# A hand-written TensorE order for the differential-attention mixer of a one-core float32 network

## The chip, the cores and the metric

The kernel is one program on one core of a Trainium2 chip. Its time is the device time of one execution, in microseconds. The core has five engines, each with its own instruction stream: TensorE (PE, matmuls and transposes), VectorE (DVE), ScalarE (ACT), GpSimd (POOL) and SyncE (SP, which issues DMAs). An engine runs its stream in order. A semaphore makes an instruction wait for another engine, and everything behind it on that engine waits too.

## The reference, cut to what matters

Two blocks with convolution, attention and feed-forward layers come first. Then a second network of two layers runs on T = 272 tokens (16 learned meta tokens and 256 real ones) of width 1024. Its first layer is a gated feed-forward, the mixer that is changed here, and another feed-forward; a sparse-attention mixer and more feed-forwards follow. The mixer is differential attention with 8 heads. Each head has two queries and two keys of width 64, and one value of width 128:

```python
def _diff_attention(h, pos, cid, w_in, qk_norm, lam, subln, lambda_init, rel_bias):
    q, k, v = jnp.split(h @ w_in, [2 * A_HEADS * A_HD, 4 * A_HEADS * A_HD], axis=-1)
    q = _rms_norm(q.reshape(bsz, t, A_HEADS, 2, A_HD), qk_norm[0])
    k = _rms_norm(k.reshape(bsz, t, A_HEADS, 2, A_HD), qk_norm[1])
    ...
        logits = jnp.einsum("bqhmd,bkhmd->bmhqk", qb, k).astype(jnp.float32) * scale + bias
        p = jax.nn.softmax(jnp.where(visible, logits, NEG_INF), axis=-1)
        pd = p[:, 0] - lam_full * p[:, 1]
        return jnp.einsum("bhqk,bkhe->bqhe", pd.astype(v.dtype), v)
    ...
    o = _rms_norm(o, subln) * (1.0 - lambda_init)
    return o.reshape(bsz, t, A_HEADS * A_VD)
...
h = h + mix @ w_out[layer]
```

Everything is float32. Chunks of 64 tokens limit what a query sees; the 16 meta queries see only the meta tokens.

## The kernel before, in words

**Dense work.** A float32 product is three matmuls (`mm3`, L212 to L214): weights and activations are each split into a high part (`wh`, `xh`) and a rest (`wl`, `xl`), and wh.xh, wh.xl and wl.xh are summed in one PSUM bank. One step is 128 x 128 weights against 272 columns. Weights stream through the kernel in a fixed plan: SP loads a chunk of 2048 columns (`raw`), ACT casts a piece of up to 1024 (`wh`, L187), DVE, or POOL for a few pieces, subtracts (`wl`, L189). `take` hands out the next piece, `ahead` splits one more, four pieces ahead of use.

**The mixer** (`diff_mix`) works head by head. `prep(h)` projects the head's queries and keys (two tiles of 8 `mm3` steps), scales them (`hx`, L831), loads two bias tiles, squares (`sq`, POOL, L843), sums squares over 64 rows by a matmul with a block of ones (L847), and normalises: two logarithms and two exponentials on ACT (L848, L849), then DVE products into `nu` (L850 to L852) and `qk` (L856). `values(h)` projects the values (8 steps), scales them into `vx` (L863), and transposes them in three pieces (L868 to L870). `attend(h)` makes the scores of both softmaxes (L220), adds the bias and takes minima (L895), exponentials on ACT, their weighted difference (L911), four transposes (`probs_t`, L977 to L980), and the product with the values (L916). After each odd head, `sub_norm` normalises a pair of heads (sum of squares by a matmul with ones, L929) and splits the result into `y`, the input of the output projection. `meta` does the same for the 16 meta queries of several heads at once.

**PSUM.** The mixer has eight banks by tag: mm 2, s 2, t 1, n 2, o 1 (L788). The tag n is used by the lambda product, each `n` sum of squares, the value transposes, the meta work, and the last pair's norm. A new bank of a tag waits until the one from two uses earlier has been read.

**The order.** The heads are written as a loop: `prep` two heads ahead (LAG = 2), `attend(h)`, `prep(h + 2)`, `values(h + 1)`. A scheduler with a model of the engines then decides each engine's final order, so that on PE the blocks of different heads lie among each other. `out_proj` (L376) takes the output projection in two passes over the eight result tiles: `WO_PASSES[2]` names the inputs (heads) of each pass, and each pass adds into the residual `X` (L388). The first pass here uses heads 0 to 5, the second 6 and 7.

## Time and profile before

| | |
|---|---|
| three runs | 1722.18, 1720.2, 1721.84 us; median 1721.84 |
| profiled execution | 1716.95 us, span 1715.2 us |
| granted TensorE clock, mean | 0.994 |
| busy share of the span | PE 98%, DVE 64%, ACT 52%, POOL 22% |
| DMA | 287.56 MB, mean 168 GB/s |
| chain that ended last | PE 92%, DVE 4%, ACT, issue and DMA 1% each |

The profile is of one execution; its span is the time between the first and the last instruction, and the execution lasts 1.75 us longer. PE is busy nearly throughout, so the places where it waits are few and can be listed. A matmul's row lasts longer than the distance to the next row, because matmuls are pipelined: costs of PE work are read from the distance of starts.

### The profile page before, as it was taken

What the parts mean: (1) busy time and instruction counts of PE and PEld (TensorE: products, weight loads), DVE (VectorE), ACT (ScalarE), POOL (GpSimd) and SP (SyncE); (2) the same over time, 40 slices, a digit from 0 to 9 for tenths busy, and PEclk for the clock granted to TensorE, in tenths of its full rate; (3) what the DMA queues carried; (4) which work ended last, traced back from release to release, by engine and by line L of the source; (5) the groups of instructions that cost most, each with busy time, mean ns of one, the idle gap of its engine ahead of it and who ended that gap; (6) DMA issues with size and microseconds to landing.
All of it is one profiled execution on the core that took longest, in us unless ns stands there. A gap on an engine that the chain in (4) does not pass through costs nothing.

```text
span 1715.2 us, 32923 instructions
## 1 busy us (share of the span) xinstructions
PE 1678.1 (98%) x13474; PEld 1633.1 (95%) x13474; DVE 1103.9 (64%) x1808; ACT 895.9 (52%) x1554; POOL 375.6 (22%) x402
## 2 busy tenths in 40 slices
PE   7999999999999999999999999999999989999999
PEld 7999999998899999999988999999999977899999
DVE  7767666565766566655788766556665576666652
ACT  6545445476544555444566544445444457754441
POOL 3013220011322013211421222211221224432210
PEclk9999999999999999999999999999999999999999
DMA  8456655432555545445642454554454333335551
GB/s 282 167 195 225 229 185 185 172 124 99 174 195 179 191 172 174 177 176 180 193 127 89 147 174 174 174 182 171 177 177 174 124 126 126 124 136 186 183 192 69
DMA packets 59495, 287.56 MB, mean 168 GB/s; under 512 B 12064, under 2 KB 22816, under 8 KB 27472
## 3 DMA queue, kind: packets, MB, share of 16 engines
q1 hardware_dynamic: 58512, 284.80, 47.6%
q8 instruction: 106, 1.74, 0.4%
q10 hardware_dynamic: 832, 0.66, 0.1%
q14 instruction: 45, 0.37, 0.1%
HBM read 284.34 MB, written 5.53 MB: 169 GB/s over the span
## 4 chain that ended last, share of the span: by engine, by line
PE 92%; DVE 4%; ACT 1%; issue 1%; DMA 1%; POOL 0%; SPq 0%; ACTq 0%; DVEq 0%; POOLq 0%
PE mm L212 21%; PE mm L213 21%; PE mm L214 21%; PE z L214 8%; PE z L212 8%; PE z L213 8%; DVE wl L189 1%; PE s L1177 1%; PE o L220 1%; PE z L220 1%; DVE xl L229 1%; PE o L916 1%; DMA X<-in_xT_dram 1%; PE s L220 1%; PE n L847 0%
## 5 line engine op out<-in xcount | busy, mean ns | idle before, releaser
L187 ACT CAST wh<-raw 128x1024 fp32r<-128x1024 f32 (+1 forms) x521 | 540.5, 1040 | 634.3 <-PE mm L213 418.2
L189 DVE TENSOR_TENSOR wl<-raw,wh 128x1024 fp32r<-128x1024 f32 (+1 forms) x513 | 631.7, 1233 | 315.3 <-ACT wh L187 312.6
L212 PE MATMUL mm<-xh,wh 128*128 128x256 f32 (+2 forms) x1768 | 510.0, 289 | 5.4 <-DVE X L388 2.2
L213 PE MATMUL mm<-xl,wh 128*128 128x256 f32 (+2 forms) x1768 | 506.1, 286 | 4.0 <-DVE xl L229 3.7
L214 PE MATMUL mm<-xh,wl 128*128 128x256 f32 (+2 forms) x1768 | 506.3, 286 | 0.0
L212 PEld LDWEIGHTS mm<-xh,wh 128*128 128x128 f32 (+1 forms) x1768 | 333.4, 189 | 11.7 <-issue 2.8
L213 PEld LDWEIGHTS mm<-xl,wh 128*128 128x128 f32 (+1 forms) x1768 | 332.8, 188 | 8.0 <-DVE xl L229 4.9
L214 PEld LDWEIGHTS mm<-xh,wl 128*128 128x128 f32 (+1 forms) x1768 | 333.6, 189 | 1.2 <-issue 0.6
L214 PE MATMUL z<-xh,wl 128*128 128x256 f32 (+1 forms) x1088 | 311.0, 286 | 0.0
L213 PE MATMUL z<-xl,wh 128*128 128x256 f32 (+1 forms) x1088 | 309.9, 285 | 0.0
L212 PE MATMUL z<-xh,wh 128*128 128x256 f32 (+1 forms) x1088 | 309.6, 285 | 0.0
L212 PE MATMUL mm<-gh,wh 128*128 128x256 f32 (+1 forms) x1056 | 300.5, 285 | 0.0
L214 PE MATMUL mm<-gh,wl 128*128 128x256 f32 (+1 forms) x1056 | 299.5, 284 | 0.0
L213 PE MATMUL mm<-gl,wh 128*128 128x256 f32 (+1 forms) x1056 | 299.5, 284 | 0.0
L344 POOL TENSOR_TENSOR es<-es,r 128x256 f32<-128x256 f32 (+1 forms) x110 | 157.1, 1428 | 483.8 <-ACT es L343 483.8
L214 PEld LDWEIGHTS z<-xh,wl 128*128 128x128 f32 x1088 | 205.5, 189 | 0.2
L212 PEld LDWEIGHTS z<-xh,wh 128*128 128x128 f32 x1088 | 205.2, 189 | 0.0
L213 PEld LDWEIGHTS z<-xl,wh 128*128 128x128 f32 x1088 | 204.8, 188 | 0.0
L213 PEld LDWEIGHTS mm<-gl,wh 128*128 128x128 f32 x1056 | 199.2, 189 | 0.0
L214 PEld LDWEIGHTS mm<-gh,wl 128*128 128x128 f32 x1056 | 198.5, 188 | 0.0
L212 PEld LDWEIGHTS mm<-gh,wh 128*128 128x128 f32 x1056 | 198.4, 188 | 0.0
L345 DVE TENSOR_TENSOR ea<-z,es 128x256 f32<-128x256 f32 (+1 forms) x132 | 57.1, 433 | 96.1 <-PE z L214 52.1
(362 smaller groups left out, 1793.3 us busy)
## 6 DMA issues: line engine op xcount, KB each, us to landing
raw<-in_gu_dram SPq DMA_DIRECT2D x132, 1024.0 KB, 4.8
raw<-in_wd_dram SPq DMA_DIRECT2D x66, 1024.0 KB, 4.8
raw<-in_wo_dram SPq DMA_DIRECT2D x13, 1024.0 KB, 4.8
raw<-in_aw_dram SPq DMA_DIRECT2D x12, 1024.0 KB, 4.8
raw<-in_a_in_dram SPq DMA_DIRECT2D x9, 1024.0 KB, 5.3
nb<-scr SPq DMA_DIRECT2D x32, 136.0 KB, 2.4
scr<-relrow SPq DMA_DIRECT2D x16, 271.5 KB, 5.2
raw<-in_mkv_dram SPq DMA_DIRECT2D x4, 1024.0 KB, 4.8
```

The lines of the kernel that those rows point to most:

```text
L187: self.nc.scalar.copy(h[:, :c], t[:, x : x + c])
L189: eng.tensor_tensor(l[:, :c], t[:, x : x + c], h[:, :c].bitcast(F32), ALU.subtract)
L212: mm(out, wh, xh, start=first, stop=False, skip_group_check=chk)
L213: mm(out, wh, xl, start=False, stop=False, skip_group_check=chk)
L214: mm(out, wl, xh, start=False, stop=last, skip_group_check=chk)
L220: self.nc.tensor.matmul(out, w, x, start=start, stop=stop, skip_group_check=True)
L229: self.nc.vector.scalar_tensor_tensor(l, src, col, h.bitcast(F32), ALU.mult, ALU.subtract)
L344: nc.gpsimd.tensor_tensor(s, s, r, ALU.mult)
L345: nc.vector.tensor_tensor(a, B[:, :cols], s, ALU.mult)
L916: nc.tensor.matmul(os[0][:, e * S + oc.start : e * S + oc.stop], v, pr[:, pc], start=e == 0 and i == 0, stop=e == 1 and i == 3, skip_group ...
L1177: nc.tensor.matmul(s[:, c], q[:, k, qc], ckg[:, k, k0 : k0 + n], start=k == 0, stop=k == 1)
```

## The change

The functions are cut in smaller ones (`project`, `normalise`, `value`, `turn`, `scores`, `probs`, `apply`, `pair_norm`, `meta_probs`, `meta_apply`, `meta_norm`), and these are called in a written sequence. While `in_order` is set, every PE instruction goes through a wrapper (`Ordered`) that keeps it in program order; in the changed kernel all PE instructions therefore carry the line L141. The other engines stay with the scheduler. The output projection takes heads 0 to 3 in its first pass and 4 to 7 in its second; the first pass's eight steps stand between the work of heads 6 and 7, and the second pass's first four tiles are done in two halves. The meta work is grouped 4 + 4 instead of 6 + 2, with its product in a bank of tag t. Outside the mixer PE's calls go through the wrapper with `in_order` off; the rest of the code is the same.

```diff
-    [[0, 1, 2, 3, 4, 5], [6, 7]],
+    [[0, 1, 2, 3], [4, 5, 6, 7]],
...
+class Ordered:
+    def __init__(self, net, eng):
+        self.net, self.eng = net, eng
+    def __getattr__(self, name):
+        f = getattr(self.eng, name)
+        def call(*args, **kw):
+            ins = f(*args, **kw)
+            if self.net.in_order:
+                self.net.tc.keep_in_program_order(ins)
+            return ins
+        return call
...
+    def wo_pass(self, i, p, y, cols, res, tags):
+        ks = WO_PASSES[i][p]
+        n = len(ks)
+        per = wo_pieces(n)
+        ws, banks = {}, {}
+        def step(m, lo=0, hi=n):
+            if not lo:
+                if m % per == 0:
+                    ws[m // per] = self.take(f"wo{i}_{p}", per * n)
+                banks[m] = self.bank(tags[m % len(tags)])
+            w = ws[m // per]
+            for j in range(lo, hi):
+                c = m % per * n + j
+                self.mm3(banks[m][:, :cols], (w[0][:, c], w[1][:, c]), (y[0][:, ks[j], :cols], y[1][:, ks[j], :cols]),
+                         j == 0, j == n - 1, chk=True)
+            if hi == n:
+                self.nc.vector.tensor_tensor(res[m], banks[m][:, :cols], res[m], ALU.add)
+                if m % per == per - 1:
+                    self.ahead()
+        return step
...
-            def prep(h):
+            def project(h):
...
+                nc.gpsimd.tensor_tensor(sq, x, x, ALU.mult)
+                qks[h] = x, sq, nbs
+            def normalise(h):
+                x, sq, nbs = qks.pop(h)
...
-            def values(h):
+            def value(h):
...
+            def turn(h):
+                vx = vxs[h % 2]
                 b = self.bank("n")[:, : 3 * P].rearrange("p (a b) -> p a b", a=3)
-                nc.tensor.transpose(b[:, 0], vx[:, 48 : 48 + P], self.ident)
-                nc.tensor.transpose(b[:, 1], vx[:, 48 + P :], self.ident)
-                nc.tensor.transpose(b[:48, 2], vx[:, :48], self.ident)
+                self.pe.transpose(b[:, 0], vx[:, 48 : 48 + P], self.ident)
+                self.pe.transpose(b[:, 1], vx[:, 48 + P :], self.ident)
+                self.pe.transpose(b[:48, 2], vx[:, :48], self.ident)
...
-            def attend(h):
+            os, qks, vs, pms, prs, sqs = {}, {}, {}, {}, {}, {}
+            def scores(h):
                 qk, nbs = qks.pop(h)
-                vr, vq = vs.pop(h)
-                e = h % 2
-                pm = []
+                pm = pms[h] = []
...
-                if h == NH - 1:
-                    meta(6, NH)
-                (L, _), (L1, s1) = pm
+            def probs(h):
+                (L, _), (L1, s1) = pms.pop(h)
                 for qc, k0, n, c, tt in SEGS:
                     nc.vector.scalar_tensor_tensor(L[:, c], L1[:, c], s1[:, 2 + tt : 3 + tt], L[:, c], ALU.mult, ALU.add)
-                pr = self.probs_t(L, pt, self.bank("t"))
+                prs[h] = self.probs_t(L, pt, self.bank("t"))
+            def apply(h):
+                vr, vq = vs.pop(h)
+                e, pr = h % 2, prs.pop(h)
...
+                    sq = self.t(pt, [P, 2 * S], "osq", bufs=1)
+                    nc.scalar.activation(sq, os[0], AF.Square)
+                    sqs[h] = os[0], sq
+            def pair_norm(h):
+                o, sq = sqs.pop(h)
+                yh, yl = (c[:, h - 1 : h + 1, NM:] for c in y)
+                sub_norm(o, sq, yh, yl, 2, S, "t" if h < NH - 1 else "n", (pt, "o", 2 * S))
...
-                o = self.bank("n")
+                prs["meta"] = ph
+            def meta_apply(h0, h1):
+                n, ph = h1 - h0, prs.pop("meta")
+                o = self.bank("t")
...
-            for h in range(LAG):
-                prep(h)
-            values(0)
-            for h in range(NH):
-                attend(h)
-                if h + LAG < NH:
-                    prep(h + LAG)
-                if h + 1 < NH:
-                    values(h + 1)
-                if h == 5:
-                    meta(0, 6)
-            self.out_proj(2, y, T, Xf, ("mm", "s"))
+                    self.pe.matmul(o[:, c], vm[:NM, h0 + h], ph[:, c], start=True, stop=True)
+                sq = self.t(self.p_ev, [P, T], "ea")[:, : n * NM]
+                nc.scalar.activation(sq, o[:, : n * NM], AF.Square)
+                sqs["meta"] = o, sq
+            def meta_norm(h0, h1):
+                sub_norm(*sqs.pop("meta"), y[0][:, h0:h1, :NM], y[1][:, h0:h1, :NM], h1 - h0, NM, "n", None)
+            project(0)
+            self.in_order = True
+            project(1)
+            normalise(0)
+            value(0)
+            normalise(1)
+            turn(0)
+            for h in range(6):
+                scores(h)
+                project(h + 2)
+                probs(h)
+                if h == 4:
+                    meta_probs(0, 4)
+                value(h + 1)
+                if h == 4:
+                    meta_apply(0, 4)
+                apply(h)
+                if h == 4:
+                    meta_norm(0, 4)
+                normalise(h + 2)
+                turn(h + 1)
+                if h % 2:
+                    pair_norm(h)
+            early = self.wo_pass(2, 0, y, T, Xf, ("mm",))
+            late = self.wo_pass(2, 1, y, T, Xf, ("s", "s", "mm", "mm"))
+            scores(6)
+            value(7)
+            early(0)
+            early(1)
+            probs(6)
+            scores(7)
+            turn(7)
+            early(2)
+            apply(6)
+            early(3)
+            early(4)
+            probs(7)
+            meta_probs(4, NH)
+            early(5)
+            meta_apply(4, NH)
+            apply(7)
+            meta_norm(4, NH)
+            pair_norm(7)
+            early(6)
+            early(7)
+            for m in range(4):
+                late(m, 0, 2)
+            for m in range(4):
+                late(m, 2, 4)
+            for m in range(4, KD):
+                late(m)
+            self.in_order = False
```

**PE, a head in the middle of the loop.** Before, the two sums of squares of one head (`n<-sq,blk`) are followed by the rest of the probabilities' transposes and by scores; the value transposes (`ident,vx0` into `n`) stand 27 rows later, behind projection steps.

```order
L847 MATMUL n_1465_10301<-sq_1462_10297,blk_93 128x272
L847 MATMUL n_1466_10306<-sq_1462_10297,blk_93 128x272
L978 MATMUL t_1446_10197<-ident_91,L10_1374_9756 128x128
L979 MATMUL t_1446_10197<-ident_91,L10_1374_9756 128x128
L980 MATMUL t_1446_10197<-ident_91,L10_1374_9756 128x128
L220 MATMUL s_1474_10358<-qk_1436_10127 128x272
...
L868 MATMUL n_1472_10350<-ident_91,vx0_1370_9752 128x128
L869 MATMUL n_1472_10350<-ident_91,vx0_1370_9752 128x128
L870 MATMUL n_1472_10350<-ident_91,vx0_1370_9752 48x128
```

Now the sums of squares of head 3 come behind the product of head 1 with its values, and the transposes of head 2's values directly behind them, ahead of head 2's scores. Of the tag n's two banks the two sums take both, and the transposes take the next.

```order
L141 MATMUL o_1434_10139<-pr_1430_10106,vm_1366_9748 128x128
L141 MATMUL o_1434_10139<-pr_1430_10106,vn0_1367_9749 128x128
L141 MATMUL n_1437_10146<-sq_1428_10097,blk_93 128x272
L141 MATMUL n_1438_10151<-sq_1428_10097,blk_93 128x272
L141 MATMUL n_1440_10162<-ident_91,vx1_1371_9753 128x128 x2
L141 MATMUL n_1440_10162<-ident_91,vx1_1371_9753 48x128
L141 MATMUL s_1443_10171<-qk_1411_9985 128x144
L141 MATMUL s_1442_10170<-qk_1411_9985 128x144
```

What moved: the transposes stand directly behind the sums of squares that use the same tag, and the next head's scores stand behind the transposes.

**PE, the last two heads.** Before, the meta norm (`n<-ea,ones`), head 6's product, head 7's probabilities and its values' transposes stand together, and the first projection step (`mm<-xh,wh`) comes after the meta transposes.

```order
L929 MATMUL n_1599_11107<-ea_1598_11105,ones_92 128x96
L916 MATMUL o_1608_11153<-pr_1607_11151,v_1593_11076 128x256
...
L916 MATMUL o_1608_11153<-pr_1607_11151,vn0_1367_9749 128x128
L977 MATMUL t_1626_11255<-ident_91,L10_1374_9756 128x128
...
L980 MATMUL t_1626_11255<-ident_91,L10_1374_9756 128x128
L868 MATMUL n_1612_11189<-ident_91,vx1_1371_9753 128x128
L869 MATMUL n_1612_11189<-ident_91,vx1_1371_9753 128x128
L870 MATMUL n_1612_11189<-ident_91,vx1_1371_9753 48x128
L950 MATMUL n_1619_11231<-ident_91,ml_1365_9746 16x16 x2
L212 MATMUL mm_1633_11282<-xh_1363_9744,wh_1576_10999 128x272
```

Now steps of the projection (`mm<-xl,wh`, `mm<-xh,wl`) stand ahead of head 6's probabilities (`L00`) and again behind the transposes of head 7's values.

```order
L141 MATMUL mm_1611_11187<-xl_1364_9745,wh_1578_11007 128x272
L141 MATMUL mm_1611_11187<-xh_1363_9744,wl_1579_11008 128x272
L141 MATMUL t_1614_11207<-ident_91,L00_1372_9754 128x128 x4
L141 MATMUL s_1617_11215<-qk_1596_11091 128x144
L141 MATMUL s_1616_11214<-qk_1596_11091 128x144
...
L141 MATMUL n_1620_11239<-ident_91,vx1_1371_9753 128x128 x2
L141 MATMUL n_1620_11239<-ident_91,vx1_1371_9753 48x128
L141 MATMUL mm_1622_11247<-xh_1363_9744,wh_1580_11011 128x272
L141 MATMUL mm_1622_11247<-xl_1364_9745,wh_1580_11011 128x272
L141 MATMUL mm_1622_11247<-xh_1363_9744,wl_1581_11012 128x272
```

What moved: the output projection's first pass has come forward from behind head 7 to between the blocks of heads 6 and 7.

**DVE, the first two heads.** Before, one head's `nu`, the values of head 0 and the second head's `nu` stand as here.

```order
L851 SCALAR_TENSOR_TENSOR nu_1387_9842<-nu_1387_9842,nt_1388_9843 128x544
L831 TENSOR_TENSOR hx_1392_9861<-mm_1395_9889,r_1359_9722 128x272
L852 SCALAR_TENSOR_TENSOR nu_1387_9842<-nu_1387_9842,nt_1388_9843 128x544
L856 SCALAR_TENSOR_TENSOR qk_1391_9857<-hx_1376_9766,gq_9740,nu_1387_9842 128x272
L856 SCALAR_TENSOR_TENSOR qk_1391_9857<-hx_1376_9766,gains_78,nu_1387_9842 128x272
L863 TENSOR_TENSOR vx0_1370_9752<-mm_1409_9958,r_1359_9722 128x272
L189 TENSOR_TENSOR wl_1439_10158<-raw_1423_10062,wh_1438_10157 128x1024
L831 TENSOR_TENSOR hx_1421_10036<-mm_1422_10037,r_1359_9722 128x272
L189 TENSOR_TENSOR wl_1457_10278<-raw_1453_10223,wh_1456_10277 128x1024
L850 SCALAR_TENSOR_TENSOR nu_1403_9937<-n_1405_9940,nt_1404_9938 128x272
```

Now, in this order:

```order
L898 SCALAR_TENSOR_TENSOR nu_1398_9920<-n_1401_9927,nt_1399_9921 128x272
L899 SCALAR_TENSOR_TENSOR nu_1398_9920<-nu_1398_9920,nt_1399_9921 128x544
L911 TENSOR_TENSOR vx0_1370_9752<-mm_1404_9940,r_1359_9722 128x272
L900 SCALAR_TENSOR_TENSOR nu_1398_9920<-nu_1398_9920,nt_1399_9921 128x544
L209 TENSOR_TENSOR wl_1433_10135<-raw_1420_10048,wh_1432_10134 128x1024
L904 SCALAR_TENSOR_TENSOR qk_1402_9934<-hx_1376_9766,gq_9740,nu_1398_9920 128x272
L904 SCALAR_TENSOR_TENSOR qk_1402_9934<-hx_1376_9766,gains_78,nu_1398_9920 128x272
L898 SCALAR_TENSOR_TENSOR nu_1407_9971<-n_1409_9973,nt_1408_9972 128x272
L898 SCALAR_TENSOR_TENSOR nu_1407_9971<-n_1410_9978,nt_1408_9972 128x272
```

What moved: DVE's stream is nearly the same; PE's transposes of head 0's values now stand behind the second head's sums of squares, which the last row here reads.

## Rows read from the trace of the kernel before

**Rows 1.** Windows: stretch, length, busy per engine (instructions), granted clock, DMA share, GB/s.

```profile
824.58:969.45 144.87, 142.42 (x1051) 129.83 (x1051) 118.13 (x287) 91.44 (x216) 36.09 (x70) 0.98 0.43 140
930.00:937.20 7.20, 5.88 (x47) 4.05 (x45) 6.62 (x24) 6.15 (x21) 1.64 (x2) 1.00 0.00 0
937.20:944.00 6.80, 5.83 (x25) 5.23 (x26) 3.99 (x17) 3.62 (x13) 0.00 (x0) 0.50 0.01 2
969.45:976.93 7.48, 5.52 (x39) 4.66 (x37) 7.48 (x11) 4.41 (x10) 7.11 (x7) 1.00 0.40 140
```

**Rows 2.** Waits of PE, 790 to 980: total us, times, longest us.

```profile
PE mm L213 <- DVE xl L229: 1.8, 2, 1.2
PE o L916 <- DVE st L902: 1.4, 1, 1.4
PE n L929 <- ACT ea L927: 0.9, 1, 0.9
```

**Rows 3.** PE's timeline, 863.9 to 864.7: start, duration, line, out<-in, shape.

```profile
864.11 0.37 PE L212 MATMUL mm<-xh,wh 128*128 128x272 f32 x1
864.32 0.28 PE L213 MATMUL mm<-xl,wh 128*128 128x272 f32 x1
864.44 0.29 PE L214 MATMUL mm<-xh,wl 128*128 128x272 f32 x1
```

**Rows 4.** Timeline of all engines, 835.9 to 839; idle time before in brackets.

```profile
836.25 1.08 PE L847 MATMUL n<-sq,blk 128*128 128x272 f32 x4
...
836.91 0.95 ACT L848 ACTIVATE nt<-n,eps 128x272 f32<-128x272 f32 x2 [0.67 <-PE n L847]
...
836.97 0.49 PE L212 MATMUL mm<-xh,wh 128*128 128x272 f32 x1
...
837.29 0.29 PE L213 MATMUL mm<-xl,wh 128*128 128x272 f32 x1
...
838.21 0.79 DVE L850 SCALAR_TENSOR_TENSOR nu<-n,nt 128x272 f32<-128x272 f32 x2 [0.71 <-ACT nt L849]
```

**Rows 5.** DVE's instructions by line, 820 to 965: count | busy, mean ns | idle before.

```profile
L189 DVE TENSOR_TENSOR wl<-raw,wh 128x1024 fp32r<-128x1024 f32 (+1 forms) x30 | 36.7, 1225 | 7.2 <-ACT wh L187 6.9
...
L850 DVE SCALAR_TENSOR_TENSOR nu<-n,nt 128x272 f32<-128x272 f32 x16 | 6.6, 430 | 2.8 <-ACT nt L849 2.8
...
L851 DVE SCALAR_TENSOR_TENSOR nu<-nu,nt 128x544 f32<-128x544 f32 x8 | 5.8, 719 | 0.1
...
L262 DVE SCALAR_TENSOR_TENSOR onr<-onr,onr 128x512 f32<-128x512 f32 x4 | 2.7, 683 | 0.1
```

**Rows 6.** Timelines of POOL and DVE: a slowed `qk` row, a free one at 853.43.

```profile
840.26 2.74 POOL L189 TENSOR_TENSOR wl<-raw,wh 128x1024 fp32r<-128x1024 f32 x1 [3.95 <-ACT wh L187]
...
840.78 2.52 DVE L856 SCALAR_TENSOR_TENSOR qk<-hx,gq,nu 128x272 f32<-128x272 f32 x1
...
853.43 0.48 DVE L856 SCALAR_TENSOR_TENSOR qk<-hx,gq,nu 128x272 f32<-128x272 f32 x1
```

**Rows 7.** DVE's timeline, first and last row of one head's softmax.

```profile
897.89 0.29 DVE L895 CUSTOM_DVE_ANT_0 L<-s,nb 128x144 f32<-128x144 f32 x1
...
900.71 0.78 DVE L911 SCALAR_TENSOR_TENSOR L<-L,st,L 128x144 f32<-128x144 f32 x2
```

**Rows 8.** Timelines of PE and DVE: last pair's norm, first and last row.

```profile
954.25 1.02 PE L929 MATMUL n<-osq,ones 128*128 128x512 f32 x2
...
962.76 0.68 DVE L225 TENSOR_TENSOR xl<-osq,xh 128x512 fp32r<-128x512 f32 x1
```

**Rows 9.** Tile sq on POOL: duration ns least/median/most, starts.

```profile
L843 POOL TENSOR_TENSOR sq<-hx x8: 1087/1117/3132, 833.5 to 920.4; 128x544 f32<-128x544 f32 x8
```

**Rows 10.** Windows: a cut block of transposes and scores, its scores, four transposes whole.

```profile
895.27:897.00 1.73, 1.73 (x18) 0.99 (x16) 0.97 (x2) 1.08 (x2) 1.73 (x3) 1.00 0.01 5
895.47:896.38 0.91, 0.91 (x10) 0.55 (x9) 0.44 (x1) 0.91 (x1) 0.91 (x2) 1.00 0.00 0
883.87:884.23 0.36, 0.36 (x7) 0.36 (x5) 0.10 (x1) 0.36 (x3) 0.00 (x0) 1.00 1.06 444
```

More of the change, by code (lines that the diff above doesn't have):

```diff
@@ L208, in mm3 @@
     def mm3(self, out, w, x, first, last, chk=False):
-        mm = self.nc.tensor.matmul
+        mm = self.pe.matmul
         wh, wl = w
@@ L219, in both @@
         for out, w, x in jobs[::-1]:
-            self.nc.tensor.matmul(out, w, x, start=start, stop=stop, skip_group_check=True)
+            self.pe.matmul(out, w, x, start=start, stop=stop, skip_group_check=True)
     def split_act(self, h, l, src):
@@ L284, in sumsq @@
         if n > 1:
-            nc.tensor.matmul(b[:, :cols], self.ones, acc[:, :cols], start=True, stop=False)
-        nc.tensor.matmul(b[:, :cols], self.ones, sq[:, :cols], start=n == 1, stop=True)
+            self.pe.matmul(b[:, :cols], self.ones, acc[:, :cols], start=True, stop=False)
+        self.pe.matmul(b[:, :cols], self.ones, sq[:, :cols], start=n == 1, stop=True)
         return b
@@ L560, in block1_mix0 @@
                 nc.gpsimd.tensor_tensor(sq, Xr[k], Xr[k], ALU.mult)
-                nc.tensor.matmul(ss[:, :S], self.ones, sq, start=k == 0, stop=k == KD - 1)
+                self.pe.matmul(ss[:, :S], self.ones, sq, start=k == 0, stop=k == KD - 1)
             r = self.t(self.p_ev, [P, T], "r", bufs=1)[:, :S]
@@ L722, in rel_table @@
             b = self.bank("o")
-            nc.tensor.matmul(b[:16, : hi - lo], nrb, oh[:, lo:hi], start=True, stop=True)
+            self.pe.matmul(b[:16, : hi - lo], nrb, oh[:, lo:hi], start=True, stop=True)
             nc.vector.tensor_copy(t[:, lo:hi], b[:16, : hi - lo])
@@ L769, in boundary_ffn @@
             for b, sq, cols in zip(ss, sums, (S, T)):
-                nc.tensor.matmul(b[:, :cols], self.ones, sq[:, :cols], start=True, stop=True)
+                self.pe.matmul(b[:, :cols], self.ones, sq[:, :cols], start=True, stop=True)
             r1 = self.t(p, [P, S], "r1")
@@ L799, in diff_mix @@
             lb = self.bank("n")
-            nc.tensor.matmul(lb[:, :2], self.ones[:64], pr, start=True, stop=True)
+            self.pe.matmul(lb[:, :2], self.ones[:64], pr, start=True, stop=True)
             le = p1.tile([P, 2], F32, name="lame")
@@ L1039, in dsa_mix @@
             ssk = self.bank("n")
-            nc.tensor.matmul(ssk[:, :T], self.blk, kq, start=True, stop=True)
+            self.pe.matmul(ssk[:, :T], self.blk, kq, start=True, stop=True)
             self.rsq(kq, ssk[:, :T], 64)
@@ L1176, in attend @@
                     for k in range(2):
[L1177 removed]
+                        self.pe.matmul(s[:, c], q[:, k, qc], ckg[:, k, k0 : k0 + n], start=k == 0, stop=k == 1)
                 for qc, k0, n, c, tt in SEGS:
```

36 lines of the change are left out of this document (14 added, 22 removed).

## The prediction

> **What bounds the kernel now.** I read the page first: TensorE (PE) is busy 98% of the span, so only a stretch in which it waits, runs at the lower clock or pays for changes of work can give time. The diff touches the second mixer alone, so next came the stretches by window [rows 1]. The mixer's projections and heads take 144.87 us, 824.58 to 969.45, at a mean clock of 0.98; the end of its output projection, with the start of the next feed-forward, takes 7.48 us. The reader is to see the third window there: 937.2 to 944.0 at granted clock 0.50, that is 1.2 instead of 2.4 GHz. In the 7.2 us before it PE did no projection step beyond the last heads' values, only transposes, scores, 16-column matmuls and sums, and was busy 5.88 us. Then came PE's waits [rows 2]: 0.9 and 1.4 us at the last head, and 1.8 us in two pieces for the next block's input. All else in the mixer is changes between small blocks. So PE's own order bounds the mixer, and DVE (118 of 144.87 us busy) is next.
>
> **The change part by part.** The matmuls stay the same in number (the order has 192 for the output projection before and after; the meta work is regrouped 4+4 for 6+2). Their order is now fixed, the projection is split 4+4 tiles, and its first pass stands between heads 6 and 7. The sum is made against the profiled execution, 1716.95 us; the median of three runs is 1721.84 us, 4.9 above it, and the difference is put on the median.
>
> Gain A, the last two heads. Early projection steps now stand where PE had none: the two waits go (0.89 + 1.40 = 2.3 us), and with them, I take it, the low clock. PE was busy 5.83 us at half speed there, so 2.9 us. Sum 5.2.
>
> Gain B, the end of the projection. The window 969.45 to 976.93 holds 39 matmul rows; at 0.126 us each (the spacing in [rows 3]) these are 4.9 us, so 2.6 us are lost, 1.8 of them in the waits named. Before, eight residual tiles are finished within eight steps of six matmuls; now four after six-matmul steps, then four after twelve-matmul steps, twice as much time for each tile's evacuation and split. I take 1.8, bounds 0 and 2.6.
>
> Gain C, fewer changes. Counted in the two orders, PE goes from three-pass matmuls to attention work and back 31 times before, 20 times now. The first three-pass matmul after attention work took 0.21 us instead of 0.126 in one row [rows 3] and 0.32 in another [rows 4]: 0.085 to 0.2 a round, with the step into the block perhaps 0.29. I take 0.2: 11 x 0.2 = 2.2, bounds 0.9 and 3.2.
>
> Loss D, the turn behind the normalisation. Six times in the loop the two norm matmuls of head h+2 are followed directly by the three transposes of head h+1's values (the order shown above). All three use the tag n, which has two banks. So the transposes take the bank of the first norm matmul, and it is free only when DVE has read it. What that takes is in [rows 4]: the pair starts at 836.25, ScalarE's two logarithms at 836.91, then its exponentials, DVE's first reading instruction at 838.21, and that lasts 0.43 [rows 5]. So 2.40 us from the first matmul to the release, while PE's own work on the pair lasts 0.72 to the next row at 836.97. Before, other work stood in the rest; now nothing does, and behind the transposes all of the next head's scores and its projection are queued on PE. Wait: 2.40 + some 0.06 for the semaphore - 0.72 to 0.92 = 1.5 to 1.7; six times 1.55 is 9.3.
>
> Loss E, the same at the start. The turn of head 0 stands directly behind the second head's norm. On DVE the first head's whole normalisation now stands before the release: from its norm matmul 1.96 us to DVE's start, then 0.86 + 1.44 for u, 0.43 for the values (the same size), 1.23 for a weight split, 0.96 for q and k (as in a free row, 0.48 each), 0.43 for the release [rows 5], less some 0.08 overlap on each of eight: 6.7 us. PE needs 0.72 + 24 x 0.126 + 0.72 and a change, 4.6. Wait 2.1. One q row took 2.52 us instead of 0.48 while GpSimd (POOL) split a weight piece for 2.74 us [rows 6]; such a piece stands here too, so the upper bound is 4.1. I take 2.4.
>
> On that the Trainium skill has a rule (SBUF — State Buffer, "two separate sides"): a GpSimd instruction and a VectorE one with two SBUF inputs exclude each other for the whole instruction. The row of 2.52 us agrees; by the rule alone E would be 4.1 and the sum 1.7 higher.
>
> Loss F, the probabilities of heads 2, 4 and 6. A plain head's softmax on DVE lasts from 897.89 to 901.49, 3.6 us [rows 7], and 48 projection matmuls (6.0 us) hide it. After a pair's norm DVE has in front of or among it the norm's four of about 0.68, the next head's u and q, k (2.4) and a weight split of 1.23 [rows 5]: 10.0 us, less overlaps 8.7. PE has from the same release on 0.3 of transposes, 0.5 of sums, 0.9 of scores and 6.0: 7.7. Wait 0 to 1.6 after overlaps; I take 0.7, three times 2.1.
>
> Loss G, the last pair. Its norm ran from 954.25 to 963.44, 9.2 us [rows 8], on a DVE that also had six adds or splits to do. Alone it is 6.5 by the same kinds of rows. Cover now: early steps 6 and 7 and the lower halves of four late tiles, 48 x 0.126 = 6.0. Wait 0.5 to 3.2; I take 1.2.
>
> Everything else is hidden: the casts and splits are fewer (8 x 1024 instead of 8 x 768 and 2 x 1024 columns), the weight chunks move a little, and DMA is busy 0.43 of the stretch; if that cover failed it would be a weight chunk's landing once, some 2 us.
>
> Sum: -5.2 - 1.8 - 2.2 + 9.3 + 2.4 + 2.1 + 1.2 = +5.8. On the median: 1721.84 + 5.8 = 1727.6 us.
>
> **The rivals.** Slower still. D's waits leave PE idle and then on transposes and small scores; the row at 937.2 shows that the clock can fall to 1.2 GHz after a stretch of waits and small work. Once would cost 2.9 as in A. And POOL's square, which the norm matmuls need, took 1.12 us in the median of eight but 3.13 at most [rows 9], beside a packed DVE; where POOL starts it late, behind memsets that wait for the bias DMA, 2.0 more would show, on one or two heads 3. So 1727.6 + 5.9 = 1733.5. For it: the window at the low clock and the row of 3.13 are both there. Against it: 4.4 us stand between the square's input and its use.
> By the skill's page on the SBUF just named, the square would be blocked whenever DVE runs two-input work. The median of 1.12 does not show it; if all six heads paid 2.0, the time would be some 1739.
>
> No change. D's pauses give DVE and ACT time to catch up, so that F and G vanish, and C has its upper price: 1721.84 + 11.7 - 5.2 - 1.8 - 3.2 = 1723.3. For it: DVE's idle time in the mixer. It decides when the six waits behind the norm are the only ones.
>
> Faster. Its place is the small blocks, which before stand cut into each other. Four transposes whole take 0.36 us; the block of 1.73 us from 895.27 on holds four and a head's scores [rows 10]. The scores have 0.91 of it in one piece and some 0.15 at its end, so the cut transposes have 0.67, 0.3 more than whole. If each of eight heads gets back 1.0 on its five kinds of blocks, that is 8.0 in place of C's 2.2, with B at 2.6 and F, G at nothing: 1721.84 + 11.7 - 5.2 - 2.6 - 8.0 = 1717.7; with D at its lower edge of 1.5, 1717.4. It decides from about 0.9 a head on; [rows 10] show a third of it, for one block.
>
> **How the numbers follow.** What this kernel's measurement can tell from no change is about 0.2%, 3.4 us: 1718.4 to 1725.3. Chances: the forecast, +2 to +9, 0.45; slower still 0.18; no change 0.18; faster 0.19. A third of the last, 0.06, falls inside 0.2%, as does the lower edge of the forecast, 0.03: faster by over 0.2% 0.13, within 0.2% 0.27, slower 0.60. The bounds of the parts (C 3.2, B 2.6 on one side; E 4.1, F 4.8, G 3.2 on the other) carry the forecast from 1723 to 1734; taking in most of the faster case, the range is 1717 to 1735.
>
> **What would show it.** In the profile of the changed kernel PE's waits would name the value transposes waiting for DVE's u some six times, 1.5 us each, and once more at the first head; the window of the last two heads would be at full clock with no wait over 0.5 us; the end of the projection would hold no wait for the next block's input, but one for the last pair's split. PE's changes would be fewer, and the mixer would take some 150 us where 144.87 + 7.48 less what is common stood. I am wrong if the transposes find their bank free: then D and E are gone, and the kernel is faster by over 5 us. I am wrong too if the low clock stays at the last heads, or comes at the first.

## The result, and the profile after

The changed kernel takes 1731.32 us in the median of four runs (1730.17 to 1732.82), the kernel before 1721.02 in four. The ratio is 1.006 with a 95% interval of 1.0043 to 1.0078: slower by 10.3 us. Forecast were 1727.6, that is 5.8 more, and the range 1717 to 1735, which holds the measured time.

The profiled executions differ by more, 1731.01 - 1716.95 = 14.1 us. Of this 3.7 stand ahead of the mixer: its lambda product starts at 830.25 before and at 833.99 after. They are not the change's, since a kernel below whose code is that of before up to there (e4) starts it at 835.29. So the mixer is compared from its own lambda product to the 300th matmul row of the next feed-forward. The windows (columns as in [rows 1]), first of before, then of after:

```profile
830.25:1013.49 183.24, 178.82 (x1332) 165.45 (x1331) 147.08 (x326) 112.61 (x247) 49.70 (x71) 0.98 0.43 142
```

```profile
833.99:1030.32 196.33, 179.77 (x1334) 164.28 (x1334) 149.76 (x325) 113.30 (x246) 45.37 (x71) 0.98 0.40 133
851.31:854.73 3.42, 3.42 (x20) 2.68 (x21) 3.35 (x14) 1.76 (x8) 0.29 (x1) 0.50 0.58 240
991.26:994.67 3.41, 3.41 (x11) 2.95 (x12) 0.87 (x3) 0.92 (x2) 0.00 (x0) 0.50 0.28 118
```

The mixer is 13.1 us longer. PE's busy time grew by 0.95 only; its idle time (length less busy) went from 4.4 to 16.6 us. The stretch at half clock is as long as before, 6.8 us, but in two pieces and at other places: right behind the first head's wait, and at the end of the projection. PE's waits from 828 to 1030 (total us, times, longest us) answer to [rows 2]:

```profile
PE n L141 <- DVE nu L898: 11.0, 7, 3.8
PE mm L141 <- DVE xl L249: 1.6, 1, 1.6
PE t L141 <- DVE L L960: 1.0, 3, 0.5
PE s L141 <- ACT xh L244: 0.7, 1, 0.7
PE o L141 <- POOL sqa L301: 0.6, 1, 0.6
PE n L141 <- ACT osq L973: 0.5, 1, 0.5
PE n L141 <- DVE nr L281: 0.4, 1, 0.4
PE s L141 <- DVE xl L245: 0.3, 1, 0.3
```

The first row is the transposes behind the sums of squares, seven times: 3.77 us at the first head, 1.37 at five heads, and 0.35 at the sixth, where the second sum itself had waited 0.44 for the meta norm (`nr`). The third row is the probabilities (L960 is L911 of before). One of the five of 1.37, from all engines' timeline behind head 1, with idle time in brackets, answers to [rows 4]:

```profile
879.11 1.08 PE L141 MATMUL n<-sq,blk 128*128 128x272 f32 x4
...
879.81 0.91 ACT L896 ACTIVATE nt<-n,eps 128x272 f32<-128x272 f32 x2
...
880.62 0.74 ACT L897 ACTIVATE nt<-nt 128x272 f32<-128x272 f32 x2
881.07 0.79 DVE L898 SCALAR_TENSOR_TENSOR nu<-n,nt 128x272 f32<-128x272 f32 x2 [0.62 <-ACT nt L897]
881.57 0.55 PE L141 MATMUL n<-ident,vx 128*128 128x128 f32 x3 [1.37 <-DVE nu L898]
```

From the first sum of squares to the transposes are 2.46 us, as forecast from [rows 4] (2.40 + 0.06). The profile books 1.37 of it as idle and 1.08 as busy; before, the next work followed 0.72 behind the pair, so 0.36 of that busy time is lost as well. The first head, from the timelines of POOL, DVE and PE, answers to [rows 6]:

```profile
844.15 2.38 POOL L209 TENSOR_TENSOR wl<-raw,wh 128x1024 fp32r<-128x1024 f32 x1
...
844.94 2.18 DVE L899 SCALAR_TENSOR_TENSOR nu<-nu,nt 128x544 f32<-128x544 f32 x1
...
850.17 0.79 DVE L898 SCALAR_TENSOR_TENSOR nu<-n,nt 128x272 f32<-128x272 f32 x2
...
850.67 0.55 PE L141 MATMUL n<-ident,vx 128*128 128x128 f32 x3 [3.77 <-DVE nu L898]
```

A DVE product that lasts 0.72 elsewhere took 2.18 beside POOL's weight split and ended 0.59 behind it. The Trainium skill's rule (SBUF — State Buffer, "two separate sides": the one blocks the other for the whole instruction) agrees with this row. The forecast's upper bound for E was 4.1; measured are 3.8 idle and 0.36.

### The profile page after: what moved, and what is told of

Same layout as the page of the kernel before. It is cut to its first block, busy times and chain, and to the rows that moved or that the text cites. A ratio compares the mean times of both kernels' runs of the same rounds, so it can differ in the third digit from the quotient of the medians.

```text
span 1729.3 us, 32906 instructions
## 1 busy us (share of the span) xinstructions
PE 1681.0 (97%) x13474; PEld 1633.9 (94%) x13474; DVE 1106.4 (64%) x1806; ACT 896.2 (52%) x1552; POOL 371.8 (21%) x402
## 4 chain that ended last, share of the span: by engine, by line
PE 89%; DVE 5%; ACT 2%; issue 1%; DMA 1%; POOL 1%; ACTq 0%; SPq 0%; DVEq 0%; POOLq 0%
PE mm L141 60%; PE z L141 24%; PE o L141 2%; DVE wl L209 1%; PE s L141 1%; PE n L141 1%; DMA X<-in_xT_dram 1%; DVE xl L249 1%; ACT wh L207 0%; PE b L141 0%; PE t L141 0%; DMA raw<-in_a_in_dram 0%; POOL sqa L301 0%; ACT nt L896 0%; DMA raw<-in_gu_dram 0%
## 5 line engine op out<-in xcount | busy, mean ns | idle before, releaser
L207 ACT CAST wh<-raw 128x1024 fp32r<-128x1024 f32 x519 | 540.1, 1044 | 640.7 <-PE mm L141 434.4
L141 PE MATMUL mm<-xh,wh 128*128 128x256 f32 (+1 forms) x1760 | 508.3, 289 | 6.9 <-DVE X L408 3.7
L141 PE MATMUL mm<-xl,wh 128*128 128x256 f32 (+1 forms) x1760 | 503.8, 286 | 2.1 <-DVE xl L249 1.9
L141 PE MATMUL mm<-xh,wl 128*128 128x256 f32 (+1 forms) x1760 | 503.2, 286 | 0.0
L141 PEld LDWEIGHTS mm<-xh,wh 128*128 128x128 f32 x1760 | 332.3, 189 | 12.7 <-ACT wh L207 4.1
L141 PEld LDWEIGHTS mm<-xl,wh 128*128 128x128 f32 x1760 | 331.8, 189 | 5.5 <-DVE xl L249 2.4
L141 PEld LDWEIGHTS mm<-xh,wl 128*128 128x128 f32 x1760 | 332.6, 189 | 0.7 <-issue 0.3
L141 PE MATMUL z<-xh,wl 128*128 128x256 f32 (+1 forms) x1088 | 311.1, 286 | 0.0
L141 PE MATMUL z<-xl,wh 128*128 128x256 f32 (+1 forms) x1088 | 311.0, 286 | 0.0
L141 PE MATMUL z<-xh,wh 128*128 128x256 f32 (+1 forms) x1088 | 310.2, 285 | 0.0
L141 PE MATMUL mm<-gh,wh 128*128 128x256 f32 (+1 forms) x1056 | 300.5, 285 | 0.0
L141 PE MATMUL mm<-gh,wl 128*128 128x256 f32 (+1 forms) x1056 | 299.5, 284 | 0.0
L141 PE MATMUL mm<-gl,wh 128*128 128x256 f32 (+1 forms) x1056 | 299.5, 284 | 0.0
L141 PEld LDWEIGHTS z<-xh,wl 128*128 128x128 f32 x1088 | 206.2, 190 | 0.1
L141 PEld LDWEIGHTS z<-xh,wh 128*128 128x128 f32 x1088 | 205.8, 189 | 0.1
L141 PEld LDWEIGHTS z<-xl,wh 128*128 128x128 f32 x1088 | 205.5, 189 | 0.2
L141 PEld LDWEIGHTS mm<-gl,wh 128*128 128x128 f32 x1056 | 199.2, 189 | 0.0
L141 PEld LDWEIGHTS mm<-gh,wl 128*128 128x128 f32 x1056 | 198.5, 188 | 0.0
L141 PEld LDWEIGHTS mm<-gh,wh 128*128 128x128 f32 x1056 | 198.3, 188 | 0.0
```

The source lines that it names most:

```text
L141: ins = f(*args, **kw)
L207: self.nc.scalar.copy(h[:, :c], t[:, x : x + c])
```

## The experiments

Runs that were taken together share runs of the kernel before on the same chip; each time is a median of 4 to 11 runs, with its ratio to before. The medians of before lie between 1720.3 and 1721.2 in all of them, so times from different sets can be compared to about a microsecond. Each profile is of one execution.

**e1_turn_bank_t.** The transposes take another bank, PE's order stays.

```diff
 def turn(h):
-    b = self.bank("n")[:, : 3 * P]...
+    b = self.bank("t")[:, : 3 * P]...
```

> The changed kernel with one word changed: the value transposes take a bank of tag t instead of n; PE's order stays as it is. Theory 'bank': the changed kernel's waits of the transposes for DVE's nu (11.0 us in 7 waits, the longest 3.8) are waits for the bank of the first sum of squares. They go; at the first head some 1.6 us remain, for the copy of the values, and the three pair norms, which use tag t too, wait some 0.5 us each for ACT's copies. 1731.3 - 11.0 + 1.6 + 1.5 = 1723.4, and some 1.7 less if the low clock of the first head goes too: 1721 to 1724. Rival 'DVE': DVE is late anyway, and its work is only waited for at another place (the probabilities' transposes, the last split): over 1727. Rival 'order': the fixed order of PE itself costs the time: 1729 to 1732.

Measured 1732.9, ratio 1.0059 [1.0046, 1.0073]. The waits for `nu` are gone, and others have come; PE's longest, 820 to 1000:

```profile
PE t L141 <- ACT vn L926: 3.7, 3, 1.2
PE t L141 <- DVE L L960: 3.5, 4, 1.2
PE s L141 <- POOL qk L905: 2.0, 1, 2.0
```

So the bank was what PE waited for, and freeing it was worth nothing: the pair norms wait for ACT's copies, the probabilities for DVE, and the first scores for `qk`, which POOL copies behind DVE's product. The time is far over the range of 'bank' and fits the rival 'DVE'.

**e2_turn_late.** The transposes are moved.

```diff
-normalise(1); turn(0)
+normalise(1)
 for h in range(6):
-    scores(h); project(h + 2); probs(h)
+    scores(h); project(h + 2); turn(h); probs(h)
     ...
-    normalise(h + 2); turn(h + 1)
+    normalise(h + 2)
 ...
+turn(6)        # behind value(7)
```

> The changed kernel with the value transposes of head h moved in the written sequence from behind the sums of squares to behind the projection of head h+2 (48 matmuls later), tag n as it is. Theory 'bank': the bank has long been read there, so all seven waits go, with the low clock of the first head: 1731.3 - 11.0 - 1.7 = 1718.6, between 1717 and 1721. Rival 'DVE': the seven pauses gave DVE time; without them the waits for the weighted difference (1.0 us in 3 now) grow to some 0.7 us at each of eight heads and the last split is later: 1723 to 1727. Rival 'order': 1729 to 1732.

Measured 1729.71, ratio 1.0042 [1.0029, 1.0056]: over the ranges of 'bank' and 'DVE', and in that of 'order'. The 11.0 us are gone, and 8.6 stand at two places where 1.0 stood. PE's waits, then the whole stretch and the window of head 2 from the pair norm to the weighted difference, then rows of PE and DVE there:

```profile
PE t L141 <- DVE L L960: 5.0, 3, 1.8
PE s L141 <- POOL qk L905: 3.6, 1, 3.6
```

```profile
835.29:1030.40 195.11, 181.90 (x1335) 167.57 (x1335) 147.00 (x325) 114.10 (x246) 52.66 (x71) 0.97 0.40 134
880.48:890.07 9.59, 7.98 (x65) 7.17 (x64) 9.51 (x28) 7.63 (x20) 1.77 (x6) 1.00 0.49 156
```

```profile
887.07 1.20 DVE L209 TENSOR_TENSOR wl<-raw,wh 128x1024 fp32r<-128x1024 f32 x1
...
889.38 0.76 DVE L960 SCALAR_TENSOR_TENSOR L<-L,st,L 128x144 f32<-128x144 f32 x2
...
889.78 0.96 PE L141 MATMUL t<-ident,L 128*128 128x128 f32 x4 [1.61 <-DVE L L960]
```

DVE is busy 9.51 of 9.59 us there, PE has 7.98 of work: the softmax stands among the pair's norm, the next head's `qk`, two `hx` and a weight split, as step F had it (8.7 against 7.7). In the changed kernel F was small because DVE had caught up while PE stood at the bank. In this execution a low clock follows the 3.57 us wait for `qk` and each of the three for the probabilities (1.60 to 1.79), for example:

```profile
853.47:856.88 3.41, 3.41 (x17) 3.41 (x17) 2.71 (x14) 1.90 (x9) 0.30 (x1) 0.50 0.41 161
891.01:894.43 3.42, 3.42 (x17) 3.42 (x17) 0.87 (x2) 0.35 (x1) 1.83 (x1) 0.50 0.63 199
```

**e3_scheduler_order.** The written order is not kept.

```diff
-            self.in_order = True
+            self.in_order = False
```

> The changed kernel with in_order off: same functions, same written sequence, same 4+4 projection and meta groups, but the scheduler decides PE's order as in the kernel before. Theory 'bank': the loss comes from where the fixed order puts the transposes, so the time is that of the kernel before or a little better, 1717 to 1723. Rival: the loss comes from the other parts (the projection in 4+4, the meta groups, the early steps), and stays: 1728 to 1732.

Measured 1720.85, ratio 0.9999 [0.9991, 1.0008]: the loss is the fixed order; the rest of the change, taken together and in the scheduler's order, costs or gives nothing that can be measured. The mixer, from the lambda product on as above:

```profile
835.41:1018.77 183.36, 178.44 (x1334) 165.58 (x1334) 148.47 (x325) 112.42 (x246) 43.52 (x71) 0.99 0.43 143
```

**e4_before_split44.** The kernel before with the projection in 4+4.

```diff
-    [[0, 1, 2, 3, 4, 5], [6, 7]],
+    [[0, 1, 2, 3], [4, 5, 6, 7]],
```

> The kernel before with WO_PASSES[2] as 4+4, all else as before. By my step B (twice as much time for each of the last tiles) the waits at the end of the projection (1.8 us) go: 1721.0 - 1.8 = 1719.2. Rival: the end is set by the last tile alone, from its last matmul to the split of X (wait 1.58 us in the changed kernel, 1.21 in the kernel before), whatever the passes are: 1721.0, within 1. In either case the low clock at the last heads may move.

Measured 1720.83, ratio 0.9993 [0.9984, 1.0002]. The waits at the end did fall, from 1.83 us (1.21 + 0.62) to 1.10 (0.29, and 0.81 for the next norm's sums), but a new one of 3.49 stands in the middle, since the second pass, which needs the last pair's split, now starts behind 96 matmuls of the first instead of 144. The rival's time was met, but not for its reason. PE's rows:

```profile
968.19 0.40 PE L212 MATMUL mm<-xh,wh 128*128 128x272 f32 x1 [3.49 <-ACT xh L224]
...
981.71 0.39 PE L213 MATMUL mm<-xl,wh 128*128 128x272 f32 x1 [0.29 <-DVE xl L229]
...
984.04 0.73 PE L285 MATMUL o<-sqa,ones 128*128 128x272 f32 x2 [0.81 <-POOL sqa L281]
```

**e5, e6, e7.** More work is put ahead of each wait of e2: at the start, in the loop, and both. The cut below is against e2.

```diff
 # e5, e7: at the start
 normalise(1)
+project(2)
 for h in range(6):
     scores(h)
-    project(h + 2)
+    if h: project(h + 2)
 # e6, e7: in the loop
-    turn(h); probs(h); value(h + 1); apply(h); normalise(h + 2)
+    value(h + 1); turn(h); probs(h); normalise(h + 2); apply(h)
 ...
 # e6, e7: at heads 6 and 7, one early step more ahead of each block
```

> As e2_turn_late, and the projection of head 2 (48 matmuls, 6.0 us) moved ahead of head 0's scores, where e2_turn_late waits 3.6 us for head 0's qk. Theory 'cover' (PE's written order leaves too little work behind each request to DVE; the bank was only the first of the waits in a row): this wait goes, with the low clock right behind it (1.7): 1729.7 - 3.6 - 1.7 = 1724.4, between 1723 and 1726; the waits of 1.6 to 1.8 us at heads 2, 4 and 6 stay. Rival 'DVE' (DVE's total of work is the bound): what is saved here is waited for at the next heads' probabilities, 1728 to 1730.

> As e2_turn_late, and in the loop the next head's values (24 matmuls, 3.0 us) moved from behind the probabilities' transposes to ahead of them, and the next sums of squares between these transposes and the product with the values; at head 6 a third early step ahead of the transposes. Theory 'cover': the waits at heads 2, 4 and 6 (1.6, 1.6, 1.8) and the low clock behind each (3 x 1.7) go, perhaps 0.3 us at the products comes at each head: 1729.7 - 5.0 - 5.1 + 2 = 1721.6, between 1720 and 1724. Rival 'DVE': the waits come back at the products or at the last split: over 1727.

> Both moves of e5_start_cover and e6_value_ahead. Theory 'cover': 1729.7 - 3.6 - 1.7 - 5.0 - 5.1 + 2 = 1716.3, between 1714 and 1719, faster than the kernel before (1721.2). Rival 'DVE': not under 1724.

Measured 1734.14, 1735.26 and 1732.5 (ratios 1.0087, 1.0084, 1.0069, each to 0.0014): the theory's ranges were missed all three times, and e5 lies over its rival's too. In e5 the wait went from `qk` to the probabilities behind it, in e7 too; in e6 the probabilities wait 0.2 in all, and `qk` 3.6 as in e2, with new waits for ACT's copies (2.4 us) and squares (2.1) and one of 1.7 at the meta work. One row of each, PE's timeline:

```profile
860.12 1.43 PE L141 MATMUL t<-ident,L 128*128 128x128 f32 x4 [5.54 <-DVE L L960]
```

```profile
881.33 1.12 PE L141 MATMUL t<-osq,ones 128*128 128x512 f32 x2 [0.69 <-ACT osq L973]
```

```profile
861.12 1.32 PE L141 MATMUL t<-ident,L 128*128 128x128 f32 x4 [4.01 <-DVE L L960]
```

In e7 DVE works from 843.7 to 861.5 with pauses of 1.05 us in all. In e5 and e7, work moved ahead of one request to DVE is work missing behind it at the next.

**e8_no_early.** The early steps are undone.

```diff
-early(0); early(1) ... early(5) among heads 6 and 7; early(6); early(7) behind pair_norm(7)
+for m in range(KD): early(m)        # all behind pair_norm(7)
```

> The changed kernel without the early steps between heads 6 and 7: the first pass of the projection stands whole behind the last pair's norm. By my step A the early steps were worth 5.2 us (2.3 of waits, 2.9 of low clock): 1731.3 + 5.2 = 1736.5, with waits and a low clock at the last heads. Rival: the written order has waits there in any case or hides them otherwise, and the early steps are worth under 2 us: 1730 to 1733.

Measured 1740.7, ratio 1.0117 [1.0103, 1.0131], 9.4 over the changed kernel. The direction is step A's, the size is more: a wait of 3.26 for head 6's probabilities, one of 1.43 ahead of head 7's, behind DVE's meta work, and two long spells at the lower clock (the second and third window). The first window is another spell, behind a wait of 1.37 at 898.07 that the changed kernel has too (897.9), there without a spell.

```profile
955.77 1.31 PE L141 MATMUL t<-ident,L 128*128 128x128 f32 x4 [3.26 <-DVE L L960]
```

```profile
899.91:903.32 3.41, 3.41 (x17) 3.41 (x16) 2.83 (x15) 2.23 (x10) 0.30 (x1) 0.50 0.14 26
954.53:961.35 6.82, 5.58 (x26) 4.05 (x27) 4.17 (x16) 2.77 (x10) 0.00 (x0) 0.50 0.00 0
964.77:971.59 6.82, 6.36 (x21) 5.06 (x21) 0.96 (x4) 1.33 (x5) 0.00 (x0) 0.50 0.01 2
```

**e9_three_ahead.** Another written order, the projections one head further ahead, the pair norm behind the next scores.

```diff
 for h in range(6):
-    scores(h); project(h + 2); probs(h); value(h + 1); apply(h); normalise(h + 2); turn(h + 1); pair_norm(h) if odd
+    scores(h); pair_norm(h - 1) if h in (2, 4); normalise(h + 2); project(h + 3); turn(h); probs(h); value(h + 1); apply(h)
 ...             # heads 6 and 7 and the packing of the weights follow
```

> All of PE's order by hand once more, but with the projections three heads ahead instead of two: scores(h), sums of squares of h+2, projection of h+3, value transposes and probabilities of h, values of h+1, product of h; pair norms behind the next scores; the weights of the projections packed in that order. In the kernel before PE has 28.75 us of work between the lambda product and the first probabilities, in the changed kernel 21.7, in e7 23.6, and DVE is done for the first probabilities some 26 to 27.6 us after the lambda product in each; here PE has some 27.3. Theory 'DVE' (DVE's queue at the start and behind each pair norm must be covered by PE work, and two heads ahead in a fixed order is too little; a moved wait only comes back): idle time of PE in the mixer falls from 16.6 to 6 or less, 1718 to 1723. Rival 'any written order' (DVE and ACT need the freedom of the scheduler's cut blocks; a written order of whole blocks leaves waits somewhere): over 1726.

Measured 1730.74, ratio 1.0057 [1.0045, 1.007]. At the probabilities of heads 0 to 4 no wait is left. But the product of heads 2, 4 and 6 now waits until the late pair norm has read the one bank of tag o (5.2 us). PE's idle time in the mixer is 14.4 us, where the theory had 6 or less; the time fits the rival. PE's longest waits, 820 to 1000:

```profile
PE o L141 <- DVE osq L987: 5.2, 3, 3.0
PE t L141 <- DVE L L960: 2.6, 4, 0.8
PE s L141 <- ACT xh L244: 2.0, 1, 2.0
PE n L141 <- POOL sq L884: 1.5, 1, 1.5
```

**e10_fixed_last_heads.** By hand from head 6 on only.

```diff
-            project(0)
-            self.in_order = True
+            project(0)
 ...
+            self.in_order = True
             scores(6)
```

> The changed kernel with PE's order left to the scheduler up to head 6, and by hand only from head 6's scores on (the early steps and the second pass). Theory: the loss sits in the loop and at the first head; the written end is worth what e8 showed or less. e3_scheduler_order (1720.9) less its waits at the last heads (1.2 + 0.4 + 0.3) and one low clock of 1.7: 1717.3, between 1715.5 and 1719.5. Rival: the end's early steps only repair waits that the written order makes itself, and the scheduler had none there worth more than a microsecond: 1720 to 1722.

Measured 1722.46, ratio 1.0011 [1.0002, 1.0019]. The theory failed, and the time lies 0.5 over the rival's range: the early steps are worth 9.4 us where the written order has made the waits, and the written end as a whole gives nothing over the scheduler's own.

**e11_turn_late_light.** e2 with less work for DVE: the two products that turn `nu` into the refined inverse root are left out.

```diff
-                stt(u, u, -0.5 / 64, t, ALU.mult, ALU.mult)
-                stt(u, u, 1.5, t, ALU.add, ALU.mult)
```

> e2_turn_late with DVE's load made lighter: the two refinement products of each head's 1/sqrt (0.72 us each, 11.5 us of DVE in all) are left out, so the normalisation is not refined. Theory 'DVE' (what moved from the bank to the probabilities and to qk in e2_turn_late is DVE's queue): the waits there, 5.0 at heads 2, 4, 6 and 3.6 at the first head, fall below 2 in all, and the low clocks behind them go: 1729.7 - 6.6 - 4 x 1.7 = 1716.3, between 1714 and 1720. Rival 'order' (the waits come from ACT, POOL or PE's own sequence): 1726 to 1730.

What is left in `nu` is (sum + 64 EPS) times the inverse root, that is 64 times the root itself, so this kernel does not normalise and is no candidate; only its time is used, and that the time does not depend on the values is assumed. Measured 1715.14, ratio 0.9968 [0.9956, 0.998], 14.6 under e2. The waits of 5.0 and 3.6 are 0 and 0.8, and the mixer has no low clock: 7.8 and 4 x 1.7 make 14.6, and the two profiled mixers differ by 14.7 (195.11 and 180.40). The whole stretch and the window of head 2:

```profile
834.06:1014.46 180.40, 175.03 (x1334) 162.08 (x1334) 134.43 (x309) 113.41 (x246) 45.37 (x71) 1.00 0.44 145
```

```profile
874.82:882.45 7.63, 7.63 (x64) 7.04 (x64) 7.57 (x25) 6.33 (x17) 0.73 (x4) 1.00 0.62 184
```

DVE is busy 7.57 us there instead of 9.51, and PE's 7.63 cover it: what DVE has to do behind the scores is what e2's order waits for at heads 2, 4 and 6. The same products were not left out in the scheduler's order. There PE's idle time in the mixer is 4.4 us and the low clock costs 3.4, so by an estimate from these rows less work for DVE could give 7.8 at most; at least 6.8 of the 14.6 belong to the fixed order.

**e12_refine_on_pool.** Part of that load taken off DVE, with the whole computation kept.

```diff
-ON_POOL |= {... % 6 == 4}
+ON_POOL |= {... % 6 == 4 and j != 5}      # one weight split from POOL to DVE
...
+  nc.scalar.activation(u[:, i], ss[:, :T], AF.Identity, scale=-0.5 / 64, bias=self.neps)   # heads 1 to 7
-  stt(u[:, i], ss[:, :T], 64 * EPS, t[:, i], ALU.add, ALU.mult)
-  stt(u, u, -0.5 / 64, t, ALU.mult, ALU.mult)
+  nc.gpsimd.tensor_tensor(u, u, t, ALU.mult)
+  nc.gpsimd.tensor_tensor(u, u, t, ALU.mult)
```

> e2_turn_late with the whole computation, and DVE's load made lighter another way: from the second head on, two of the four refinement products of the 1/sqrt go to POOL (two of 128x544, some 1.1 us each by the squares of that size) and their first term to ACT (0.42 us more for each half); one weight split beside the first head's norm goes from POOL to DVE. DVE loses 7 x 1.58 = 11.1 us and gains 1.2. Theory 'DVE': as e11_turn_late_light (1715.1), with some 1.5 us at the first head that e11 did not have and one low clock of 1.7: 1718.3, between 1715 and 1721. Rival 'port': POOL's products slow the DVE instructions beside them (0.72 to 2.18 us and 0.48 to 2.52 in single rows) and the waits stay: 1723 to 1730.

Measured 1730.73, ratio 1.0051 [1.0038, 1.0065]: no gain over e2, but not for the rival's reason, since nearly all of DVE's instructions kept their lengths (`qk` 0.49 in the mean; one split `xl` took 1.58 instead of 0.69). At head 2, from the timelines of ACT, DVE and PE:

```profile
881.18 0.49 ACT L896 ACTIVATE nt<-n,eps 128x272 f32<-128x272 f32 x1 [0.40 <-PE n L141]
...
883.31 0.70 ACT L267 ACTIVATE onr<-t,eps 128x512 f32<-128x512 f32 x1
...
883.54 0.31 DVE L951 CUSTOM_DVE_ANT_0 L<-s,nb 128x144 f32<-128x144 f32 x1 [2.10 <-PE s L141]
...
884.58 0.40 ACT L954 ACTIVATE L<-L,st 128x144 f32<-128x144 f32 x1
...
890.06 1.26 DVE L209 TENSOR_TENSOR wl<-raw,wh 128x1024 fp32r<-128x1024 f32 x1
...
891.24 0.77 DVE L967 SCALAR_TENSOR_TENSOR L<-L,st,L 128x144 f32<-128x144 f32 x2
...
891.65 0.33 PE L141 MATMUL t<-ident,L 128*128 128x128 f32 x1 [1.57 <-DVE L L967]
```

The products taken away stood ahead of the softmax, where DVE now idles 2.10 us. What stands between the softmax and its weighted difference (the last refinement, `qk`, the norm, a split) is still there, and ACT's longer list comes ahead of the norm's logarithm and the exponentials. So taking work from DVE is not enough by itself; why, is read from these rows and was not tested. Untested too is DVE's own order, which the scheduler makes: the weight split at 890.06 lasts 1.26 us and stands directly ahead of the weighted difference, for which PE waits 1.57; in e2 one of 1.20 stands among its last rows (887.07). No version with the whole computation beats the kernel before.

## Why the prediction was right, and where its sizes were off

The direction held, and the waits that the forecast named stand in the trace. That they are what the change costs did not hold (D and E below), and the size did not come from the terms as they were written. Over the median of the forecast, 1721.84, the measured time is 9.5 us, outside the +2 to +9 of the likeliest case: what came lies between that case and "slower still", with the low clock of the latter but without the late squares on POOL that it also named (no sum of squares waits for POOL). It is inside the range because the range is 18 us wide. On the compared stretch (13.1 us):

| step | forecast | measured | from |
|---|---|---|---|
| A, waits of the last two heads | -2.3 | -2.3 | both waits gone |
| A, low clock there | -2.9 | +0.5 | 6.8 us at half clock before and after; PE busy 5.83 and 6.83 of it |
| B, end of the projection | -1.8 | +0.3 | 1.6 + 0.6 where 1.8 stood |
| C, fewer changes | -2.2 | -2.1 | the rest of busy time: +0.95 - 0.5 (low clock) - 7 x 0.36 = -2.1 |
| D, turn behind the norm | +9.3 | +9.4 | 11.0 - 3.8 = 7.2 idle (5 x 1.37 and 0.35), and 6 x 0.36 |
| E, the same at the start | +2.4 | +4.2 | 3.8 idle and 0.36 |
| F, probabilities | +2.1 | +1.0 | three waits |
| G, last pair | +1.2 | +1.1 | 0.74 + 0.33 |
| meta and pair norm | 0 | +0.9 | 0.5 + 0.4 |

The terms sum to 13.0, 7.2 over the forecast's 5.8, most of it from the low clock (3.4), B (2.1) and E (1.8). That they come out at the 13.1 of the stretch shows nothing by itself, since C is what is left over; it was not tried by itself, but the traces hold the 31 and 20 changes that the forecast counted. The profiled pair differs by 14.1: 3.7 ahead of the stretch, 13.1 in it, and 2.7 given back behind it (701.7 us to the span's end before, 699.0 after). Ahead and behind, executions of the same code differ by as much: from the lambda product's 830.25 to 836.53, and from 698.8 to 703.1 us behind the stretch, in the fourteen profiles. The medians differ by 10.3, and the runs do not show where the other 2.8 of the 13.1 went.

**Right as waits.** D by the bank and the 2.46 us from the first sum of squares to the transposes; that the sum is met to 0.1 us is partly luck, since five of the six cost 1.73 where 1.55 was taken, and the sixth 0.7. E near its upper bound, with a DVE row slowed beside POOL's weight split as was named for it, though the row is a `nu` product with 1.46 us more and not a q row with 2.04. G.

**Wrong: D and E as the cost.** The forecast said that with the transposes' bank free the kernel would be faster than before by over 5 us. In e1 the transposes have another bank, and in e2 they stand where theirs has long been read; the kernel takes 1732.9 and 1729.71, still 11.7 and 8.5 over before. The waits of D and E hid other ones, for DVE, ACT and POOL, that the sum had only in small parts (F and G).

**Wrong: the low clock in A.** The step took the half clock as a property of the last two heads that goes with their waits. It went there and came at the first head, behind the 3.77 us wait, and at the end. The forecast had named a low clock at the first head as a sign of being wrong; it stood under "slower still", which had 0.18. All eight kernels that wait 1.97 us or more at the first head have one there (the last section), so it belonged to the likeliest case as soon as E stood in the sum.

**Wrong: B.** The step took it that more time for each tile ends the waits. In e4 they fell by 0.7 of the 1.8, and 3.49 us of waiting came in the middle of the projection; in the changed kernel the last tile's split is waited for as before (1.58).

**Half right: F.** Measured small, but only beside D. The "no change" rival said so, and e2 showed the price behind it: with D gone, F is 5.0 and not 2.1. Taking the seven waits of D and E away gave 1.6 us (e2) or nothing (e1).

**A sum.** The forecast's lower edge of 1723 does not come from B and C at their bounds, as it says (1725.8); it takes F and G at theirs too.

What the runs settle: the 10 us are the fixed order of PE (e3), and e2's waits in it hang on what DVE has to do (e11). Which part of that counts, the amount of work or its place in DVE's order, is argued from rows (e2, e12) and not shown. Nor do the runs show that no written order can be as good; those tried over the whole mixer with the full work (the changed kernel, e1, e2, e5 to e9 and e12) lie between 1729.7 and 1740.7.

## What to carry to other kernels

Before an order is fixed by hand, add up, for every place where PE waits for another engine, what that engine has queued behind the request and what PE has queued ahead of the wait. Here, at head 2 of e2, DVE had 9.5 us against PE's 8.0; in the scheduler's order (e3), which cuts the blocks into each other, no wait for the weighted difference is left. When a wait is removed, expect the next one in that engine's queue: test by making the engine's work lighter, not only by moving the wait, and look at what stands directly ahead of the answer in that engine's own order.
